# Up and down projection of a decoder layer: one chain of steps that pairs products of neighbouring units

## The chip, the cores and the metric

One core of a Trainium2 chip runs the whole layer. The metric is the device time of one execution in microseconds. Engines are named as the profile names them: PE (TensorE), DVE (VectorE), ACT (ScalarE), POOL (GpSimd) and SP, whose queue issues the DMAs.

## The reference, cut to what matters

The kernel computes one layer of a hybrid decoder for a prompt of 1024 tokens and 8 x 4 sample tokens, 1056 tokens in all. RMSNorm, w_in, the S5 branch, the attention and the gates are untouched by the change. The rest is:

```python
mixed = g_attn * (attn @ p['w_attn_o']) + g_ssm * (ssm @ p['w_ssm_o'])
x = x + mixed @ p['w_out']                                   # 1024 x 1024
hdn = jax.nn.relu(_rmsnorm(x, p['norm2_g']) @ p['w_up'])     # 1024 x 4096
x = x + (hdn * hdn) @ p['w_down']                            # 4096 x 1024
```

## The kernel before

All is fp32 and feature-major: a tile has 128 features on the partitions and T = 1056 tokens along its rows, TH = 528 in each half. An operand of a matmul is split into a rounded part and a rest (hi and lo, ACT's cast and DVE's subtraction), and each product term takes three matmuls (L1068 to L1070).

**w_out** (L1020 to L1045). Eight tiles `m` of 128 features, in the order 0 to 7. Each takes 72 matmuls of 352 columns, then DVE adds the result to x (L1034), ACT squares it (L1035), POOL adds up the squares for the norm (L1037) and the tile `x2_m` is written to `x2_d` (L1038). The left halves of the tiles fill slots 0 and 2 (L1040, L1041).

**up** (L1120 to L1158). The 1024 x 4096 product is cut into 16 units. A unit is one 2 x 2 block product with seven block products instead of eight: sums of the operand's blocks stand in seven *slots* (hi and lo, four tiles `j` each), sums of a unit's weight blocks in seven weight tiles. `prep_sums` loads the four blocks `f` of a unit and makes the sums on POOL (L946 to L949), `prep_split` splits the seven tiles `fw` on ACT (L960) and DVE (L961). `product` is 24 matmuls of 264 columns. The products of a unit go into four pairs of PSUM banks: 0, 3 and 6 one after the other into one bank pair (A or B, in turn), 2 into the other of these, 1 and 4 into C, 5 into D. In up ACT copies intermediate sums into `ua`, `ub`, DVE combines them into the four quarters of two tiles h (L1130), then come the token rsqrt with relu (L1148), the square (L1149), four POOL sums `hc`, `hd` (L1153 to L1156), and seven writes to `h_d` (L1158), since the sums of h are down's slots.

Slots 0 to 3 lie in `slot_hi` and `slot_lo`, slots 4 to 6 in `slot_b`, whose pool opens after w_out. All fills except those of slots 0 and 2 (sums `t`, casts L1090 and L1093, subtractions L1091 and L1094) stand in a loop after w_out (L1098 to L1111). `token_rsqrt_bcast` (L1160) turns the sum of squares into `r2`: matmuls `n_ss` (L150), a chain of small DVE operations (L137 to L154), two diagonal tiles (L161, L165), and matmuls `n_pb` (L169).

**down** (L1187 to L1214). 16 units again: four groups `g` of 1024 hidden features, four pairs `mp` of output tiles in each. All four units of a group use the same seven slots. `load_group` (L1173 to L1185) reads them from `h_d`: 14 transfers `st`, each with an ACT cast (L1184) and a DVE subtraction (L1185), through six staging tiles. The old x comes back as eight tiles `y` (L1168), and DVE adds each product into their quarters (L1194), eight such additions in a unit.

The order on each engine is set by a scheduler at build time, from the order of the program text and the priorities that `high_priority` gives; each engine then runs its own list in that order and waits on semaphores. Four things of the text matter here:

```python
for j in range(4):                 # after w_out: all fills but slots 0 and 2
    ...
for p in range(16):
    up(p, w0 if p == 0 else prep_split(prep_sums(F_UP + p), W5))
for g in range(4):
    load_group(g)                  # all seven slots between two units
    for mp in range(4):
        down(g, mp, prep_split(prep_sums(F_DN + 4 * g + mp), W3))
```

Of the kernel before, what the change touches and what calls it, by code (L numbers as in the profile page):

```python
# [58 lines left out]
def trunk_kernel(ctx, tc, xt, wts, wff, pp_d, cp_d, g1_d, abias, sbias, ckt, cvr, ck_tail, cv_tail,  # L59
# [862 lines left out]
    with ExitStack() as ph2:  # L922
# [16 lines left out]
        def prep_sums(u, ahead=4000):
            with tc.high_priority(offset=ahead):  # L940
                raw = [fwp.tile([P, 512], F32, tag="wr", bufs=7, name=f"f{u}_{i}") for i in range(4)]
                for i in (2, 3, 0, 1):
# [7 lines left out]
            return u, (a11, a21, a12, s2, a22, s4, s1)  # L950

        def prep_split(us, tags, ahead=4000):
            u, xs = us
            out = []
            with tc.high_priority(offset=ahead):
                for i, x in enumerate(xs):
                    tag = tags[_wn[0] % len(tags)]
                    _wn[0] += 1
                    w = (accp if tag[0] == "a" else wpool).tile([P, 2, 512], F32R, tag=tag, name=f"fw{u}_{i}")
                    A.copy(w[:, 0], x)  # L960
                    V.tensor_sub(w[:, 1], x, w[:, 0].bitcast(F32))  # L961
                    out.append(w)
            return out

        with ExitStack() as phs:
# [54 lines left out]
            for m in range(8):  # L1020
                w = load_unit(U_OUT + m)
                x2 = accp.tile([P, T], F32, tag=f"a{m}", name=f"x2_{m}") if m < 4 else (
                    newT if m < 7 else newT2)(f"x2_{m}")
# [4 lines left out]
                if m == 0:
                    gemm_k([blk(w, k) for k in range(8)], macts, pss)
                for c in range(3):  # L1030
                    s = chunks[c]
                    if m:
# [15 lines left out]
        with ExitStack() as phs:
# [8 lines left out]
            def tmp(i, name):  # L1057
                return fp_.tile([P, 2, TH], F32, tag=f"tm{i}", name=name)
# [19 lines left out]
            def halves(t):  # L1078
                return hv(t[:, :TH]), hv(t[:, TH:])

            W3 = ("whi", "wlo", "wraw")
            W5 = ("whi", "wlo", "wraw", "a0", "a1", "whi", "wlo", "wraw", "a2", "a3")
            w0 = prep_split(w0, W3, 1000)
            _wn[0] = 0
            g2n = cpool.tile([P, 8], F32, name="g2n")
            V.tensor_scalar(g2n, C("g2"), -1.0, None, ALU.mult)
            def fill(r, j, src, scale=None):
                hi, lo = slots[r][0][:, j], slots[r][1][:, j]
                if scale is None:
                    A.copy(hi, src)  # L1090
                    V.tensor_sub(lo, src, hi.bitcast(F32))  # L1091
                else:
                    A.activation(hi, src, AF.Copy, scale=scale)  # L1093
                    V.scalar_tensor_tensor(lo, src, scale, hi.bitcast(F32), ALU.mult, ALU.subtract)  # L1094

            for j in range(4):
                xa, xb = x2s[j], x2s[4 + j]
                ga, gb = C("g2", j, j + 1), C("g2", 4 + j, 5 + j)  # L1098
                gan = g2n[:, j : j + 1]
                q1, q2, q3 = [tmp(i, f"t{j}_{i}") for i in range(3)]  # L1100
                b22, t1, t2, t3, t4 = q1[:, 0], q1[:, 1], q2[:, 0], q2[:, 1], q3[:, 0]
                A.activation(b22, xb[:, TH:], AF.Copy, scale=gb)
                V.scalar_tensor_tensor(t3, xa[:, TH:], gan, b22, ALU.mult, ALU.add)
                fill(1, j, t3)
                G.tensor_add(t1, xa[:, :TH], xa[:, TH:])
                V.scalar_tensor_tensor(t2, t1, gan, b22, ALU.mult, ALU.add)
                fill(3, j, t2)
                V.scalar_tensor_tensor(t4, xb[:, :TH], gb, t2, ALU.mult, ALU.add)
# [288 lines left out]
```

## Time and profile before

| | |
|---|---|
| median of 3 runs | 1420.46 us (1417.52 to 1422.59) |
| the profiled execution | 1419.88 us |
| its span | 1418.1 us |
| mean granted clock of TensorE | 0.972 |
| PE, DVE, ACT, POOL busy | 95%, 62%, 36%, 31% of the span |
| up and down, from the last matmul of w_out to the end of the last product | 705.2 to 1413.7 us |

Busy PE is not the same as PE at its peak. The useful number is the cadence of matmuls in a stretch that nothing disturbs, and how far the other stretches fall behind it.

### The profile page before, as it was taken

What the parts mean: (1) busy time and instruction counts of PE and PEld (TensorE: products, weight loads), DVE (VectorE), ACT (ScalarE), POOL (GpSimd) and SP (SyncE); (2) the same over time, 40 slices, a digit from 0 to 9 for tenths busy, and PEclk for the clock granted to TensorE, in tenths of its full rate; (3) what the DMA queues carried; (4) which work ended last, traced back from release to release, by engine and by line L of the source; (5) the groups of instructions that cost most, each with busy time, mean ns of one, the idle gap of its engine ahead of it and who ended that gap; (6) DMA issues with size and microseconds to landing.
All of it is one profiled execution on the core that took longest, in us unless ns stands there. A gap on an engine that the chain in (4) does not pass through costs nothing. (4 is left out here: it accounts for less than half of the span.)

```text
span 1418.1 us, 23479 instructions
## 1 busy us (share of the span) xinstructions
PE 1347.4 (95%) x9405; PEld 1272.7 (90%) x9405; DVE 881.4 (62%) x1401; ACT 505.3 (36%) x843; POOL 442.4 (31%) x348
## 2 busy tenths in 40 slices
PE   7989999999989999999959999999987999999998
PEld 7978999999866659999949999999987999999998
DVE  7969567333467556543497566656657586775953
ACT  6112233223165453222344444434435252432520
POOL 5595322000000000004345665566542233232320
PEclk9999999999989999999969999999998999999999
DMA  6232442331321115423203444344469262452531
GB/s 256 92 86 74 117 89 85 101 114 53 116 92 53 54 44 202 163 92 133 93 8 124 165 152 151 123 159 153 149 240 342 84 234 78 123 183 58 167 107 62
DMA packets 88909, 176.31 MB, mean 124 GB/s; under 512 B 23296, under 2 KB 32512, under 8 KB 88512
## 3 DMA queue, kind: packets, MB, share of 16 engines
q1 hardware_dynamic: 88800, 174.81, 38.1%
q8 instruction: 74, 1.21, 0.3%
q14 instruction: 35, 0.29, 0.1%
HBM read 121.37 MB, written 53.23 MB: 123 GB/s over the span
## 5 line engine op out<-in xcount | busy, mean ns | idle before, releaser
L118 PE MATMUL z<-x_hi,whi 128*128 128x352 f32 x528 | 173.4, 328 | 1.8 <-DVE gs L250 1.8
L120 PE MATMUL z<-x_hi,wlo 128*128 128x352 f32 x528 | 172.2, 327 | 1.5 <-DVE wlo L105 1.5
L119 PE MATMUL z<-x_lo,whi 128*128 128x352 f32 x528 | 172.5, 327 | 0.0
L1037 POOL TENSOR_TENSOR ssq<-ssq,sq 128x352 f32<-128x352 f32 x21 | 23.8, 1135 | 435.1 <-ACT sq L1035 435.1
L960 ACT CAST fw<-f 128x512 fp32r<-128x512 f32 x128 | 79.4, 622 | 167.1 <-PE Dd L1070 34.1
L961 DVE TENSOR_TENSOR fw<-f,fw 128x512 fp32r<-128x512 f32 x128 | 110.8, 867 | 40.8 <-ACT fw L960 40.8
L946 POOL TENSOR_TENSOR f_s<-f,f 128x512 f32<-128x512 f32 x32 | 53.3, 1665 | 217.4 <-DVE fw L961 175.8
L961 DVE TENSOR_TENSOR fw<-f_s,fw 128x512 fp32r<-128x512 f32 x96 | 92.3, 962 | 28.1 <-ACT fw L960 28.0
L120 PEld LDWEIGHTS z<-x_hi,wlo 128*128 128x128 f32 x528 | 99.9, 189 | 4.3 <-issue 2.3
L118 PEld LDWEIGHTS z<-x_hi,whi 128*128 128x128 f32 x528 | 100.5, 190 | 3.1 <-ACT whi L104 2.1
L119 PEld LDWEIGHTS z<-x_lo,whi 128*128 128x128 f32 x528 | 100.6, 191 | 1.7 <-issue 1.3
L104 ACT CAST whi<-wraw 128x1024 fp32r<-128x1024 f32 (+3 forms) x46 | 46.5, 1011 | 153.0 <-PE z L119 90.9
L960 ACT CAST fw<-f_s 128x512 fp32r<-128x512 f32 x96 | 59.7, 621 | 109.2 <-PE Cd L1070 32.3
L105 DVE TENSOR_TENSOR wlo<-wraw,whi 128x1024 fp32r<-128x1024 f32 (+3 forms) x46 | 57.9, 1260 | 12.9 <-ACT whi L104 12.8
L118 PE MATMUL wo<-m_hi,whi 128*128 128x352 f32 x192 | 61.9, 323 | 0.0
L119 PE MATMUL wo<-m_lo,whi 128*128 128x352 f32 x192 | 61.5, 320 | 0.0
L120 PE MATMUL wo<-m_hi,wlo 128*128 128x352 f32 x192 | 61.5, 320 | 0.0
L1068 PE MATMUL Ad<-slot_hi,fw 128*128 128x264 f32 x192 | 56.6, 295 | 4.8 <-ACT slot_hi L1184 3.3
L1153 POOL TENSOR_TENSOR hc<-h 128x528 f32<-128x528 f32 x16 | 21.8, 1363 | 120.9 <-ACT h L1149 120.9
L1069 PE MATMUL Ad<-slot_lo,fw 128*128 128x264 f32 x192 | 56.4, 294 | 2.0 <-DVE slot_lo L1185 2.0
L949 POOL TENSOR_TENSOR f_s<-f_s,f 128x512 f32<-128x512 f32 x32 | 50.6, 1581 | 21.2 <-issue 15.1
L1068 PE MATMUL Au<-slot_hi,fw 128*128 128x264 f32 x192 | 56.2, 293 | 0.7 <-ACT ua L1130 0.7
(420 smaller groups left out, 4647.4 us busy)
## 6 DMA issues: line engine op xcount, KB each, us to landing
f<-in_dram SPq DMA_DIRECT2D x128, 256.0 KB
st<-h_d SPq DMA_DIRECT2D x56, 528.0 KB
wraw<-in_dram SPq DMA_DIRECT2D x42, 512.0 KB
h_d<-h SPq DMA_DIRECT2D x48, 264.0 KB
g_d<-gs SPq DMA_DIRECT2D x16, 528.0 KB
h_d<-hc SPq DMA_DIRECT2D x32, 264.0 KB
h_d<-hd SPq DMA_DIRECT2D x32, 264.0 KB
gr<-y_d SPq DMA_DIRECT2D x8, 528.0 KB
```

What stands on the lines that cost most here:

```text
L104: A.copy(whi[:, s], raw[:, s])
L105: V.tensor_sub(wlo[:, s], raw[:, s], whi[:, s].bitcast(F32))
L118: mm_(out, wh, ah[:, s], start=first, stop=False)
L119: mm_(out, wh, al[:, s], start=False, stop=False)
L120: mm_(out, wl, ah[:, s], start=False, stop=last)
L946: G.tensor_add(s1, a21, a22)
L949: G.tensor_add(s4, s2, a12)
L960: A.copy(w[:, 0], x)
L961: V.tensor_sub(w[:, 1], x, w[:, 0].bitcast(F32))
L1037: G.tensor_add(sacc[:, s], sacc[:, s], sq[:, s])
L1068: mm_(o, wh, ah[:, j, s], start=start and j == 0, stop=False, **k)
L1069: mm_(o, wh, al[:, j, s], start=False, stop=False, **k)
```

## The change

1. The w_out tiles go in the order 0, 4, 1, 5, 2, 6, 3, 7. After a tile of the first four, slots 0 and 6 of that `j` are filled; after a tile of the last four, slots 3 and 1, and `t4`, the operand of slot 4, is written to memory (`t4_d`) because slot 4 lies in the pool that opens later. `slot_hi` now holds slots 0, 6, 3, 1. After w_out only slots 2, 4 (from `t4_d`) and 5 are left to fill.
2. Up and down become 33 steps. Step n runs products 0, 3, 6 of unit n and products 1, 2, 4, 5 of unit n-1, in the order 0, 1', 2', 3, 4', 5', 6 (with a prime those of the unit before). The number of products and of matmuls is the same.
3. The evacuations of up write straight into h, without `ua` and `ub`: four ACT copies and four DVE operations a unit, as before.
4. Down's slots 0, 3, 6 of a group are loaded in the first step of the group, slots 1, 2, 4, 5 in the second, each when its last reader is done. Staging: three `tm` tiles and two others (before: four and two); the tiles `hc`, `hd` share those three. The tiles `y` are loaded two per step.
5. Two of a unit's four weight blocks, needed a step later, lie in a pool of their own of four tiles.

```diff
-            for m in range(8):
+            for i, m in enumerate((0, 4, 1, 5, 2, 6, 3, 7)):
...
+                if m < 4:
+                    fill_a(0, j, xa[:, :TH], ga)
+                    G.tensor_add(t1, xa[:, :TH], xa[:, TH:])
+                    fill_a(6, j, t1, ga)
+                else:
+                    q2 = newT2(f"q2_{j}")
+                    t2, t3 = q2[:, :TH], q2[:, TH:]
+                    with tc.high_priority(offset=40):
+                        A.activation(b22, xb[:, TH:], AF.Copy, scale=gb)
+                        V.scalar_tensor_tensor(t2, t1, gan, b22, ALU.mult, ALU.add)
+                        fill_a(3, j, t2)
+                    V.scalar_tensor_tensor(t3, xa[:, TH:], gan, b22, ALU.mult, ALU.add)
+                    fill_a(1, j, t3)
+                    V.scalar_tensor_tensor(t2, xb[:, :TH], gb, t2, ALU.mult, ALU.add)
+                    nc.sync.dma_start(t4_d[j], t2)
...
-            def tmp(i, name):
-                return fp_.tile([P, 2, TH], F32, tag=f"tm{i}", name=name)
+            def tmp(name):
+                return fp_.tile([P, 2, TH], F32, tag="tm", bufs=3, name=name)
...
+            order = ((0, 0), (1, 1), (1, 2), (0, 3), (1, 4), (1, 5), (0, 6))
+            banks = {0: "X", 1: "C", 2: "Y", 3: "X", 4: "C", 5: "D", 6: "X"}
...
+            def step(n, first, second, tags, ahead=4000):
...
+                for side, r in order:
+                    item = (first, second)[side]
+                    if not item:
+                        continue
+                    k = banks[r]
+                    start = r not in (3, 4, 6)
+                    if start:
+                        ps[k] = psd(tag[k], f"{k}{n}")
+                    product(ps[k], ws[r], r, start)
+                    item["ev"](r, pv(ps[k]))
+                if second and second.get("end"):
+                    second["end"]()
...
             for p in range(16):
-                up(p, w0 if p == 0 else prep_split(prep_sums(F_UP + p), W5))
+                cur = up_item(p)
+                if p:
+                    prep_sums(F_UP + p, fp_)
+                step(p, cur, prev, W6 if p in (0, 15) else W10, 4000 if p else 1000)
+                if p == 0:
+                    r2 = newT2("r2")
...
+                    token_rsqrt_bcast(cpool, lambda n: psd("D", n)[:, 0, :], sacc, dg, r2, "n2")
+                prev = cur
...
-            for g in range(4):
-                load_group(g)
-                for mp in range(4):
-                    down(g, mp, prep_split(prep_sums(F_DN + 4 * g + mp), W3))
+            for n in range(17):
+                cur = None
+                if n < 16:
+                    cur = down_item(n)
+                    if n % 4 == 0:
+                        load_slots(n // 4, (0, 3, 6))
+                    prep_sums(F_DN + n, fp_)
+                if n % 4 == 1:
+                    load_slots(n // 4, (1, 2, 4, 5))
+                step(16 + n, cur, prev, W6)
+                prev = cur
```

The lists of the engines up to w_out are the same in both kernels. Three places show what moved.

ACT at the end of w_out, before (`sq27` is the square of the last tile, L1040 a cast of the w_out loop, L1090 and L1093 the casts of slots after it):

```order
L1035 ACTIVATE sq27_6080<-x2_7_6078 128x352 x2
L1040 ACTIVATE slot_hi_5386<-x2_7_6078,cp_152 128x528
L960 CAST fw0_3_6186<-f0_s1_5970 128x512
L960 CAST fw0_4_6189<-f0_3_5964 128x512
L1102 ACTIVATE t0_0_6200<-x2_4_5775,cp_152 128x528
L1035 ACTIVATE sq27_6080<-x2_7_6078 128x352
L1093 ACTIVATE slot_b_6176<-t0_0_6200,cp_152 128x528
L1090 CAST slot_b_6176<-t0_0_6200 128x528
L1090 CAST slot_hi_5386<-t0_1_6201 128x528 x2
L1102 ACTIVATE t1_0_6218<-x2_5_5871,cp_152 128x528
L960 CAST fw0_6_6195<-f0_s0_5969 128x512
L1090 CAST slot_b_6176<-t0_2_6202 128x528
```

and now (`L1029`, `L1032` are the casts of slots, `fw0` the weights of the first unit):

```order
L1029 CAST slot_hi_5387<-q2_2_5990 128x528 x2
L1058 ACTIVATE sq23_6024<-x2_3_6021 128x352 x2
L1032 ACTIVATE slot_hi_5387<-x2_3_6021,cp_153 128x528
L964 CAST fw0_0_6260<-f0_0_6000 128x512
L964 CAST fw0_3_6263<-f0_s1_6009 128x512
L1058 ACTIVATE sq23_6024<-x2_3_6021 128x352
L1032 ACTIVATE slot_hi_5387<-q1_3_6022,cp_153 128x528
L1058 ACTIVATE sq27_6123<-x2_7_6121 128x352 x2
L964 CAST fw0_2_6420<-f0_1_6001 128x512
L1032 ACTIVATE slot_b_6227<-x2_4_5494,cp_153 128x528
L1032 ACTIVATE slot_b_6227<-x2_5_5698,cp_153 128x528
L1032 ACTIVATE slot_b_6227<-x2_6_5902,cp_153 128x528
```

Before, only slots 0 and 2 were complete at the last square, and 23 casts and copies for the other slots followed (the three sums `t1`, `t2`, `t3` of each `j` among their inputs). Now the casts of slots 3 and 0 stand among the squares, and after the last tile follow those of slot_b, which need no sum.

The DMA queue where up passes into down, before (`y` are the old x, `h_d` the sums of h, `st0_r j` the loads of slot r for the first group):

```order
L1168 DMA y0_10079<-x2_d_76 128x1056
L1158 DMA h_d_77<-hc14_9829 128x528
L943 DMA f17_1_10368<-in_2_dram 128x512
L1158 DMA h_d_77<-hd14_9830 128x528
L1168 DMA y1_10081<-x2_d_76 128x1056
L1158 DMA h_d_77<-hd14_9830 128x528
L1168 DMA y3_10085<-x2_d_76 128x1056
L1183 DMA st0_00_10095<-h_d_77 128x1056
L1168 DMA y4_10087<-x2_d_76 128x1056
L1168 DMA y5_10089<-x2_d_76 128x1056
L1183 DMA st0_02_10099<-h_d_77 128x1056
```

and now:

```order
L1182 DMA h_d_77<-h14_0_9452 128x528
L1182 DMA h_d_77<-hc14_9909 128x528
L1221 DMA st0_00_9926<-h_d_77 128x1056
L1182 DMA h_d_77<-hc14_9909 128x528
L1232 DMA y5_10437<-x2_d_76 128x1056
L1182 DMA h_d_77<-hd14_9910 128x528
L1221 DMA st0_02_9930<-h_d_77 128x1056
L1221 DMA st0_32_9938<-h_d_77 128x1056
L1182 DMA h_d_77<-hd14_9910 128x528
L1221 DMA st0_30_9934<-h_d_77 128x1056
L950 DMA f18_2_10441<-in_2_dram 128x512
```

Five of the eight loads `y` are now ahead of this place (y0 to y4), and slots 0, 3 and 6 come first among the loads; they still stand behind the writes of h14.

DVE at the first change of group, before (L1185 slots, L961 weights, L1194 additions into y):

```order
L1185 TENSOR_TENSOR slot_lo_5387<-st1_12_11027,slot_hi_5386 128x1056
L1185 TENSOR_TENSOR slot_lo_5387<-st1_20_11031,slot_hi_5386 128x1056
L1194 TENSOR_TENSOR y6_10091<-y6_10091,Ad0_3_10836 128x528
L961 TENSOR_TENSOR fw20_1_11089<-f20_2_11073,fw20_1_11089 128x512
L1185 TENSOR_TENSOR slot_lo_5387<-st1_22_11035,slot_hi_5386 128x1056
L1185 TENSOR_TENSOR slot_lo_5387<-st1_30_11039,slot_hi_5386 128x1056
L1194 TENSOR_TENSOR y7_10093<-y7_10093,Bd0_3_10835 128x528
L961 TENSOR_TENSOR fw20_2_11092<-f20_1_11072,fw20_2_11092 128x512
L1185 TENSOR_TENSOR slot_lo_5387<-st1_32_11043,slot_hi_5386 128x1056
L1185 TENSOR_TENSOR slot_b_6176<-st1_40_11047,slot_b_6176 128x1056
L961 TENSOR_TENSOR fw20_3_11095<-f20_s1_11080,fw20_3_11095 128x512
L1194 TENSOR_TENSOR y7_10093<-y7_10093,Cd0_3_10837 128x528
```

and now (L1223 slots, L965 weights, L1125 additions):

```order
L1223 TENSOR_TENSOR slot_lo_5388<-st1_30_10883,slot_hi_5387 128x1056
L1125 TENSOR_TENSOR y7_10657<-y7_10657,X19_10695 128x528
L965 TENSOR_TENSOR fw19_2_10920<-f19_1_10660,fw19_2_10920 128x512
L1223 TENSOR_TENSOR slot_lo_5388<-st1_32_10887,slot_hi_5387 128x1056
L1125 TENSOR_TENSOR y5_10437<-y5_10437,C19_10721 128x528
L965 TENSOR_TENSOR fw20_3_10923<-f20_s1_10908,fw20_3_10923 128x512
L1125 TENSOR_TENSOR y4_10435<-y4_10435,D19_10823 128x528
L965 TENSOR_TENSOR fw19_4_10926<-f19_3_10662,fw19_4_10926 128x512
L1223 TENSOR_TENSOR slot_lo_5388<-st1_60_10891,slot_hi_5387 128x1056
L1125 TENSOR_TENSOR y7_10657<-y7_10657,X19_10695 128x528
L1125 TENSOR_TENSOR y6_10655<-y6_10655,X19_10695 128x528
L965 TENSOR_TENSOR fw19_5_10929<-f19_s2_10669,fw19_5_10929 128x512
```

Before, six of these twelve are subtractions of a slot, two for every weight tile. Now there are three beside four weight tiles, with additions of two products of one unit (C19, D19 belong to unit 18) and of the next (X19) between them.

## Rows read from the trace of the kernel before

**Rows 1.** The page, section 2: busy tenths of TensorE, and the clock granted to it in tenths of full speed, in 40 slices of the span (35.5 us each):

```profile
PE   7989999999989999999959999999987999999998
...
PEclk9999999999989999999969999999998999999999
```

**Rows 2.** Busy time by stretch of the span (us from its start): the length, then busy us (and instructions) of PE, its weight loads, DVE, ACT and POOL, the granted clock (1.00 is full speed), the DMA share and GB/s. The stretches in order: w_out; the start of up; the worst part of that start; up; the passage from up to down; 10 us of that passage; the first change of group with two stretches of 10 us (1150 and 1160) beside it; the second and the third change; down after the last change:

```profile
613.60:705.20 91.60, 91.60 (x577) 91.43 (x576) 32.48 (x46) 25.89 (x45) 27.77 (x24) 1.00 0.31 107
705.20:750.00 44.80, 28.45 (x169) 26.17 (x169) 39.16 (x61) 21.67 (x37) 17.28 (x9) 0.70 0.11 34
720.00:737.00 17.00, 4.73 (x14) 3.21 (x14) 15.04 (x28) 10.08 (x16) 6.07 (x2) 0.50 0.06 15
750.00:1040.00 290.00, 290.00 (x2398) 290.00 (x2398) 180.91 (x190) 119.62 (x191) 173.86 (x116) 1.00 0.44 145
1040.00:1105.00 65.00, 53.78 (x373) 50.44 (x372) 41.23 (x42) 27.21 (x33) 23.04 (x15) 0.87 0.91 316
1060.00:1070.00 10.00, 6.53 (x24) 5.54 (x24) 5.47 (x6) 4.75 (x5) 2.85 (x3) 0.51 0.92 291
1150.00:1160.00 10.00, 10.00 (x85) 10.00 (x84) 10.00 (x12) 6.46 (x9) 0.00 (x0) 1.00 0.89 310
1155.00:1180.00 25.00, 22.77 (x187) 22.56 (x187) 22.94 (x28) 9.89 (x13) 8.56 (x4) 1.00 0.79 278
1160.00:1170.00 10.00, 7.77 (x64) 7.56 (x63) 10.00 (x12) 4.83 (x6) 6.14 (x3) 1.00 1.01 380
1230.00:1262.00 32.00, 29.77 (x234) 29.56 (x233) 29.75 (x33) 16.20 (x21) 9.49 (x5) 0.95 0.81 274
1320.00:1345.00 25.00, 22.77 (x176) 22.56 (x176) 23.83 (x27) 11.06 (x14) 8.54 (x4) 0.93 0.48 165
1345.00:1410.00 65.00, 65.00 (x540) 65.00 (x539) 30.65 (x45) 11.80 (x19) 10.33 (x8) 1.00 0.26 87
```

**Rows 3.** The timeline of PE (start, length, operation, and in brackets the idle time before it and what ended it): three rows from the last matmul of w_out to the first matmul of the token rsqrt's broadcast, then one of the passage from up to down:

```profile
705.00 0.32 PE L120 MATMUL wo<-m_hi,wlo 128*128 128x352 f32 x1
...
729.82 0.59 PE L1068 MATMUL Cu<-slot_hi,fw 128*128 128x264 f32 x1 [5.19 <-ACT slot_hi L1090]
...
745.88 0.32 PE L169 MATMUL n_pb<-diag,ones 128*128 128x352 f32 x1
...
1060.59 0.59 PE L1068 MATMUL Ad<-slot_hi,fw 128*128 128x264 f32 x1 [2.48 <-ACT slot_hi L1184]
```

**Rows 4.** The timeline of the start of up, one row of POOL and seven of DVE, then one of DVE at the first change of group (columns as in group 3):

```profile
712.03 1.74 POOL L948 TENSOR_TENSOR f_s<-f_s,f 128x512 f32<-128x512 f32 x1
712.56 1.77 DVE L1091 TENSOR_TENSOR slot_b<-t,slot_b 128x528 fp32r<-128x528 f32 x1
...
717.32 0.68 DVE L961 TENSOR_TENSOR fw<-f_s,fw 128x512 fp32r<-128x512 f32 x1
...
728.34 0.76 DVE L1103 SCALAR_TENSOR_TENSOR t<-x,g2n,t 128x528 f32<-128x528 f32 x1
...
729.70 0.70 DVE L1091 TENSOR_TENSOR slot_b<-t,slot_b 128x528 fp32r<-128x528 f32 x1
730.32 1.32 DVE L141 TENSOR_TENSOR n_t<-n_i 128x9 f32<-128x9 f32 x1
...
741.41 1.22 DVE L161 TENSOR_TENSOR diag<-cp,n_yh 128x1024 fp32r<-128x1024 f32 x1
...
743.83 0.23 DVE L165 TENSOR_SCALAR diag<-cp,n_yl 128x32 fp32r<-128x32 f32 x1
...
1156.52 1.24 DVE L1185 TENSOR_TENSOR slot_lo<-st,slot_hi 128x1056 fp32r<-128x1056 f32 x1
```

**Rows 5.** The timeline of the DMA queue in the passage from up to down (start, time to issue, line, transfer):

```profile
1040.89 0.36 SPq L1168 DMA_DIRECT2D y<-x_d  x1
...
1053.11 0.32 SPq L1183 DMA_DIRECT2D st<-h_d  x1
...
1060.17 0.32 SPq L1183 DMA_DIRECT2D st<-h_d  x1
```

**Rows 6.** Groups of instructions, five of DVE and one of ACT from 705 us to the end, one of POOL from 600 us: line, engine, operation, shapes, count, then busy us and mean ns of one, then the idle time before them and what ended it:

```profile
L961 DVE TENSOR_TENSOR fw<-f,fw 128x512 fp32r<-128x512 f32 x125 | 108.8, 871 | 40.1 <-ACT fw L960 40.1
L961 DVE TENSOR_TENSOR fw<-f_s,fw 128x512 fp32r<-128x512 f32 x95 | 91.6, 964 | 27.4 <-ACT fw L960 27.3
L1185 DVE TENSOR_TENSOR slot_lo<-st,slot_hi 128x1056 fp32r<-128x1056 f32 x32 | 46.8, 1485 | 8.8 <-ACT slot_hi L1184 8.8
L1148 DVE SCALAR_TENSOR_TENSOR h<-h,r 128x1056 f32<-128x1056 f32 x32 | 41.1, 1320 | 0.0
...
L1194 DVE TENSOR_TENSOR y<-y,Ad 128x528 f32<-128x528 f32 x40 | 27.4, 699 | 31.8 <-PE Ad L1070 31.8
...
L1184 ACT CAST slot_hi<-st 128x1056 fp32r<-128x1056 f32 x32 | 33.5, 1073 | 13.2 <-DMA st<-h_d 10.9 <-PE Bd L1070 2.3
...
L947 POOL TENSOR_TENSOR f<-f,f 128x512 f32<-128x512 f32 x32 | 50.5, 1579 | 1.4
```

**Rows 7.** PE's waits from 1150 to 1180 us (us in total, times, longest):

```profile
PE Dd L1070 <- DVE fw L961: 2.2, 1, 2.2
```

**Rows 8.** The timeline of the end, the last row of DVE and of the DMA queue (columns as in groups 3 and 5):

```profile
1413.72 1.32 DVE L1194 TENSOR_TENSOR y<-y,Bd 128x528 f32<-128x528 f32 x2 [2.20 <-PE Bd L1070]
...
1414.46 0.94 SPq L1214 DMA_DIRECT2D out_dram<-y  x2
```

More of the change, by code (lines that the diff above doesn't have):

```diff
@@ L181, in trunk_kernel @@
     h_d = dpool.tile([7, P, 16, TH], F32, name="h_d")
+    t4_d = dpool.tile([4, P, TH], F32, name="t4_d")
     psx = ctx.enter_context(ExitStack())
@@ L949, in prep_sums, with split_w @@
                 G.tensor_add(s4, s2, a12)
[L950 to L954, printed above, removed]
+            raws[u] = (a11, a21, a12, s2, a22, s4, s1)
+        def split_w(u, i, tags, ahead=4000):
             with tc.high_priority(offset=ahead):
[L956 to L963, printed above, removed]
+                x = raws[u][i]
+                tag = tags[_wn[0] % len(tags)]
+                _wn[0] += 1
+                w = (accp if tag[0] == "a" else wpool).tile([P, 2, 512], F32R, tag=tag, name=f"fw{u}_{i}")
+                A.copy(w[:, 0], x)
+                V.tensor_sub(w[:, 1], x, w[:, 0].bitcast(F32))
+            return w
         with ExitStack() as phs:
@@ L1076, in hv @@
                 return ap.rearrange("p (c t) -> p c t", c=2)
[L1078 to L1094, printed above, removed]
@@ L1096, in trunk_kernel @@
-            for j in range(4):
[L1097 to L1108, printed above, removed]
-                fill(4, j, t4)
-                fill(5, j, b22)
-                fill(6, j, t1, ga)
@@ L1160, in trunk_kernel, with quads @@
[L1160 to L1169 removed]
+            def quads(ta, tb):
+                return [hv(t[:, h * TH : (h + 1) * TH]) for t in (ta, tb) for h in range(2)]
@@ new lines, in trunk_kernel @@
+            for j in range(4):
+                fill(slots[2][0][:, j], slots[2][1][:, j], xbs[j][:, :TH], C("g2", 4 + j, 5 + j))
+            t4s = [tmp(f"t4_{i}") for i in range(2)]
+            for j in range(4):
+                t4 = t4s[j // 2][:, j % 2]
+                nc.sync.dma_start(t4, t4_d[j])
+                fill(slots[4][0][:, j], slots[4][1][:, j], t4)
+            for j in range(4):
+                fill(slots[5][0][:, j], slots[5][1][:, j], xbs[j][:, TH:], C("g2", 4 + j, 5 + j))
@@ L1171, in trunk_kernel, with load_slots @@
+            accs = {}
             _sn = [0]
-            def load_group(g):
+            def load_slots(g, rs):
                 with tc.high_priority(offset=1500):
-                    for r in range(7):
+                    for r in rs:
                         hi, lo = slots[r]
```

222 lines of the change are left out of this document (124 added, 98 removed).

## The prediction

> **What bounds the kernel now.** I read the slices of the page first. PE is near its full tenths everywhere in the second half of the span but in two places, about 700 to 750 us and 1030 to 1100 us, and the granted clock dips there too [rows 1]. Next come the stretches: up from 750 to 1040 us and down after 1345 us show PE busy without a gap at clock 1.00, so PE bounds them. The cadence of the last of them is 65 / 540 = 0.1204 us for a matmul of 264 columns, so a product of 24 costs 2.89 us and seven of them 20.2 us. In w_out a matmul of 352 columns takes 91.6 / 577 = 0.159 us, also without a gap [rows 2]. The change leaves the 32 x 7 x 24 = 5376 matmuls of up and down as they are, so all that it can give back is what the other stretches lose against that cadence. By matmul counts [rows 2]:
>
> - start of up: 44.8 - 169 x 0.1204 = 24.5 us
> - up to down: 65 - 373 x 0.1204 = 20.1 us
> - three changes of group: 25 - 187 x 0.1204 = 2.5, then 32 - 234 x 0.1204 = 3.8 and 25 - 176 x 0.1204 = 3.8, together 10.1 us
>
> That is 54.7 us, the ceiling of the gain apart from the tail. Now what ends last in each. At the start of up PE waits for ACT's casts of slots, the longest time 5.2 us, and the clock falls to 0.50, the lower of the two levels (1.2 and 2.4 GHz), when PE has stood for most of 720 to 737 us [rows 2, 3]. DVE is busy 39.2 of the 44.8 us: fills, weight splits and the token rsqrt queue on one engine [rows 2]. The diagonal tiles are done at 744 us, 39 us after w_out's last matmul, and the first `n_pb` follows at 745.9 [rows 3, 4]. In the passage PE waits for casts of loaded slots at half clock, while the DMA share is 0.91 and eight `y` loads stand in one queue with the first slot loads [rows 2, 3, 5]. At the first change of group DVE is busy 10.00 of 10 us twice and PE waits 2.2 us for a weight tile behind the slots [rows 2, 7].
>
> **The change, part by part.**
>
> *More work inside w_out: nothing.* For each `j`, DVE gets six fill operations of 528 (0.70 to 0.76 us, [rows 4]) in place of the one of slot 2, over four `j` some 14 us, ACT about 10 us and POOL four sums. They join 32.5, 25.9 and 27.8 us of work under 91.6 us of matmuls [rows 2]: DVE would come to 47. The cover is w_out itself; without it these are the very operations that PE waits for now. If two w_out tiles ran into their PSUM banks, at most one addition of 0.5 us would be late, and I take 0.
>
> *Start of up.* In the new list of DVE 46 operations stand between the last addition of w_out and the last diagonal part: 10 weight splits at 0.68, 11 slot operations with a scale at 0.76, 6 without at 0.70, the small ones 3.5 us with one of 1.32, the diagonals 2 x 1.22 + 2 x 0.23 = 2.9 [rows 4]. The 0.68 is a split beside no sum of POOL (the means 0.87 and 0.96 of [rows 6] contain the delayed ones). Sum: 6.8 + 8.4 + 4.2 + 3.5 + 2.9 = 25.8 us. A fill beside a POOL sum took 1.77 instead of 0.70 [rows 4], 1.07 us more, and POOL has nine operations in its list there (two units' sums and the last square). So the diagonals are done between 26 us (none meets) and 36 us (all do) after w_out; I take 32, since now too the sums come early. PE has 144 matmuls of 264 columns ahead of the first `n_pb`, 17.3 us, and 1 to 2 us of `n_ss`. It then stands 32 + 2 - 19 = 15, and I add 1 for the `t4` that go through memory. Loss 16 instead of 24.5: **-8.5**. Ends: diagonals at 26 us, loss 9 or 10, **-15**; at 36 us with later waits of slot 4 behind, loss 21, **-3**. Late next: the rsqrt, no longer the slots.
>
> *Up to down.* Five products of up's last two units need no load of down, 14.5 us of cover that did not exist, since all seven slots were replaced between two units. In the new order slots 0, 3 and 6 have a whole step, 20.2 us, from their last reader. Against this: the first loads stand in the queue behind the writes of h14, whose POOL sums (four at about 1.6, [rows 6]) follow two rsqrt operations of 1.32 us [rows 6] and two squares: 6.4 + 2.6 us, and with squares and write about 13 us after that unit's last product, and `st` waits for `hc`, `hd` in the three shared staging tiles. 13 us, a load (0.54 MB at the passage's 316 GB/s, 1.7 us), a cast of 1.1 and a subtraction of 1.5 us [rows 2, 6], less the 14.5 us of cover, leave some 3 or 4 us for the first product, and as much for the slots of the second step; I take 8 instead of 20.1: **-12**. Ends: 3 and 16, **-17** and **-4**. The eight `y` are spread, two a step, which takes five of them, 2.7 MB, out of the fullest 30 us and is part of this.
>
> *Changes of group.* DVE had the work of a whole group change in one step: 14 slots x 1.4, 7 splits x 0.9, 8 additions x 0.70, some 31 us against 20.2 of PE. Now it is two steps: 14 x 1.4 + 14 x 0.9 + 16 x 0.70 = 43.4 against 40.4 (for the slots between the 1.24 of an undisturbed one and the mean of 1.49, [rows 4, 6]). The 3 us can be carried over the next step, where DVE has 8 free. I take 0.5 for each change instead of 3.4: **-8.6**. Ends: no loss, **-10**, and half of today's, **-5**.
>
> *Tail.* Now the last product ends with two additions, 1.32 us, then the output goes out [rows 8]; the new last product is number 5, with one: **-0.6**.
>
> *The chain itself: 0.* Between the copy out of a bank and the next start in it lie at least two products, 5.8 us, for a copy of about 0.7; the split weights run six to ten tiles ahead as before. At the ends: nothing gained, and up to 0.2 us a step lost (33 steps, 6 us) if the queue's order delays weight loads.
>
> Sum: -8.5 - 12 - 8.6 - 0.6 = -29.7 us, from the profiled execution's 1419.9 to **1390.2 us**; that execution lies 0.6 us under the median of the runs, so I say 1391.
>
> **The rivals.**
>
> 1. *Everything hides.* Passage and changes lose nothing and the diagonals come at 26 us: -15 - 20 - 10 - 0.6 = -46, about **1374**. For it: 14.5 us of cover and PE as the only bound in 290 us of up [rows 2]. Against it: the DVE sum at the start and the queue behind h14.
> 2. *Half of it.* The start saves 3, the passage 4 and the changes 5, with the tail -13: **1407**. For it: DVE already runs 90% there, and loads share 0.91 of the DMA.
> 3. *DVE becomes the bound, slower.* Let every POOL sum hold a DVE operation for 1.07 us, as at 712 us [rows 4]. Two steps around a change then have 14 x 1.24 + 14 x 0.68 + 16 x 0.70 + 8 x 1.07 = 46.6 us of DVE against 40.4: 6.2 us late at each change, 3 us worse than now, and in the passage, where the rsqrt operations and eight sums of `hc`, `hd` come on top, up to 17 us more, so 25 there instead of 20. It decides from 43.8 us of DVE in two steps, where the loss equals today's. With the start saving 3: 9 + 5 - 3 = +11, less the tail, **1430**. The Trainium skill's page "SBUF — State Buffer", section "Who interferes with whom", has such a rule: a DVE instruction with two inputs in SBUF and a GpSimd instruction that reads SBUF share a port pair, and whichever comes second waits for the whole of the first; by that rule alone this case would be the forecast. The pair at 712 us agrees. Against its size: in the change of group at 1150 us POOL ran 0.00 of the 10 us in which DVE was full, because its sums wait for the splits, and the mean split, 0.87 to 0.96, is only a fifth to a quarter of 1.07 above 0.68 [rows 2, 6].
> 4. *The change does not do what it says*: the lists let the stalls return a step later, in sum as before, **1420**. The lists show products and loads alternating, so little speaks for it.
>
> **How the numbers follow.** The forecast's case (saving 20 to 38 us, 1382 to 1400) gets 0.60, rival 1 0.12, rival 2 0.18, rival 3 0.06, rival 4 0.04. A measurement tells 0.3%, 4.3 us, from no change, so faster 0.60 + 0.12 + 0.18 = 0.90, same 0.04, slower 0.06. The range leaves out rivals 3 and 4 and the lower half of rival 1: from 1374 to 1409, with the forecast's ends and rival 2 inside.
>
> **What would show it.** Right: the first `n_pb` about 34 us after w_out's last matmul and PE waiting there for DVE's diagonals, not for casts of slots; in the passage less than 10 us lost and no stretch of 10 us at clock 0.50; DVE under 10.00 of 10 us at the changes, and no wait of PE above 1 us there; up and down otherwise at 0.1204 us a matmul. Wrong: a wait that recurs at every step (weights behind the queue), a passage that still loses 20 us with PE waiting for `st`, or DVE operations of 1.77 us throughout the chain.

## The result

The changed kernel took 1388.94 us (median of 4 runs, 1388.26 to 1389.93) against 1420.55 us before: a ratio of 0.978, 95% interval 0.9761 to 0.9798, 31.6 us less. The forecast was 1391. Its profiled execution took 1389.93 us, span 1388.1 us, mean granted clock 0.984 instead of 0.972.

The page's slices of PE and of its clock, to set beside [rows 1]:

```profile
PE   7979999999999999999989999999997999999998
...
PEclk9999999999989999999999999999999999999999
```

The trough at slice 20 (counted from 0) is shallower, the one at slice 30 is still there, and from slice 12 on none is below 0.9 of the clock. In what follows, every loss is counted in one way: from the end of w_out's last matmul 55 us on (the start), 1020 to 1120 us (the passage), 1120 to 1370 us (the changes of group); length less 0.1204 us for each matmul. Before, these are 24.7, 20.2 and 11.2 us, up to 1.1 above the sums from [rows 2] because the stretches are longer. Stretches of the changed kernel (columns as in [rows 2]; w_out ends at 704.63 us):

```profile
704.63:759.63 55.00, 48.31 (x351) 47.25 (x350) 45.09 (x64) 28.32 (x49) 25.64 (x17) 0.91 0.39 123
1020.00:1120.00 100.00, 91.18 (x714) 89.63 (x714) 74.60 (x81) 40.05 (x54) 42.07 (x26) 0.97 0.67 224
1120.00:1370.00 250.00, 250.00 (x2071) 250.00 (x2070) 187.53 (x225) 93.06 (x126) 66.54 (x44) 1.00 0.43 134
```

55 - 351 x 0.1204 = 12.7, 100 - 714 x 0.1204 = 14.0, 250 - 2071 x 0.1204 = 0.7 us. So the start gave 12.0 us, the passage 6.2, the changes 10.5; the tail (from DVE's last additions, below) 0.8; w_out ended 0.5 us earlier. Together 30.0, which is 1419.88 - 1389.93. PE's waits from 600 us on (total, times, longest):

```profile
PE X L1105 <- DVE y L1125: 4.8, 2, 2.8
PE X L1105 <- ACT h L1125: 3.3, 2, 2.2
PE X L1105 <- ACT slot_hi L1222: 2.2, 1, 2.2
PE n_pb L169 <- DVE diag L165: 1.9, 1, 1.9
PE X L1105 <- ACT fw L964: 1.5, 1, 1.5
```

No wait of 5 us is left, and the longest are for additions of DVE into y, a kind that before shows once, 1.5 us long. At the start, PE's rows that waited (answering to 729.82 and 745.88 of [rows 3]):

```profile
711.85 0.39 PE L1105 MATMUL X<-slot_hi,fw 128*128 128x264 f32 x1 [2.21 <-ACT h L1125]
...
716.42 0.98 PE L150 MATMUL n_ss<-cp,ssq 128*128 128x1 f32 x8 [0.34 <-POOL ssq L1060]
...
729.88 0.39 PE L1105 MATMUL X<-slot_hi,fw 128*128 128x264 f32 x1 [1.07 <-ACT h L1125]
...
735.22 0.40 PE L169 MATMUL n_pb<-diag,ones 128*128 128x352 f32 x1 [1.92 <-DVE diag L165]
```

The 2.2 us and 1.1 us are for the copies out of the first unit's bank pair; the broadcast starts at 735.22, 30.6 us after w_out. The stretch up to there (columns as in [rows 2]):

```profile
704.63:735.22 30.59, 23.90 (x165) 22.84 (x163) 29.52 (x46) 18.84 (x33) 15.28 (x9) 0.89 0.47 147
```

30.59 - 165 x 0.1204 = 10.7 us, so most of the start's 12.7 us is lost here. In the passage:

```profile
1050.34 0.59 PE L1105 MATMUL X<-slot_hi,fw 128*128 128x264 f32 x1 [2.19 <-ACT slot_hi L1222]
...
1058.31 0.36 PE L1105 MATMUL X<-slot_hi,fw 128*128 128x264 f32 x1 [2.81 <-DVE y L1125]
...
1066.35 0.36 PE L1105 MATMUL X<-slot_hi,fw 128*128 128x264 f32 x1 [2.00 <-DVE y L1125]
...
1084.41 0.39 PE L1105 MATMUL X<-slot_hi,fw 128*128 128x264 f32 x1 [1.53 <-ACT fw L964]
```

The first is for the second half of slot 0, the next two for banks that DVE has not emptied. Busy time there in 5 us, and at the three changes in 30 us (columns as in [rows 2]):

```profile
1040.00:1045.00 5.00, 5.00 (x43) 4.96 (x42) 2.58 (x4) 2.12 (x3) 3.31 (x3) 1.00 0.95 320
1045.00:1050.00 5.00, 3.15 (x26) 2.93 (x25) 2.42 (x4) 0.78 (x1) 0.00 (x0) 1.00 0.96 350
1055.00:1060.00 5.00, 2.19 (x19) 2.01 (x18) 5.00 (x6) 2.72 (x4) 5.00 (x3) 1.00 1.00 364
1060.00:1065.00 5.00, 4.35 (x36) 4.13 (x35) 5.00 (x3) 2.37 (x4) 4.84 (x4) 1.00 1.03 339
1130.00:1160.00 30.00, 30.00 (x251) 30.00 (x250) 30.00 (x34) 15.11 (x19) 9.95 (x6) 1.00 0.70 223
1210.00:1240.00 30.00, 30.00 (x251) 30.00 (x250) 29.88 (x32) 15.86 (x21) 10.45 (x7) 1.00 0.72 225
1290.00:1320.00 30.00, 30.00 (x251) 30.00 (x250) 29.41 (x33) 16.29 (x20) 12.09 (x8) 1.00 0.45 139
```

From 1040 to 1050 us the DMA engines are full and DVE is half idle; ten us later DVE is full and PE waits. At the changes DVE is about as full as before ([rows 2], 1150 and 1160 us), 29.4 to 30.0 of 30 us, but PE loses nothing and the wait of [rows 7] is gone. The end of the kernel, DVE's last row, answers to [rows 8]:

```profile
1384.49 0.70 DVE L1125 TENSOR_TENSOR y<-y,D 128x528 f32<-128x528 f32 x1 [1.25 <-PE D L1107]
```

One addition instead of two; from its start to the end of the span 3.6 us instead of 1418.1 - 1413.72 = 4.4.

### The profile page after: what moved, and what is told of

Its sections match the earlier page's. It is cut to its first block, busy times and chain, and to the rows that moved or that the text cites. A ratio compares the mean times of both kernels' runs of the same rounds, so it can differ in the third digit from the quotient of the medians.

```text
span 1388.1 us, 23493 instructions
## 1 busy us (share of the span) xinstructions
PE 1336.7 (96%) x9405; PEld 1265.8 (91%) x9405; DVE 894.6 (64%) x1401; ACT 505.7 (36%) x843; POOL 433.3 (31%) x348
## 4 chain that ended last, share of the span: by engine, by line
PE 76%; DVE 7%; DMA 3%; issue 2%; ACT 1%; POOL 1%; SPq 0%; DVEq 0%; ACTq 0%; POOLq 0%
PE X L1105 6%; PE X L1106 6%; PE X L1107 6%; PE C L1106 4%; PE C L1105 4%; PE C L1107 4%; PE z L118 4%; PE z L119 4%; PE z L120 4%; PE wo L118 2%; PE wo L119 2%; PE wo L120 2%; PE D L1105 2%; PE D L1106 2%; PE D L1107 2%; PE Y L1106 2%
## 5 line engine op out<-in xcount | busy, mean ns | idle before, releaser
L1105 PE MATMUL X<-slot_hi,fw 128*128 128x264 f32 x768 | 221.5, 288 | 12.5 <-DVE y L1125 4.8
L1107 PE MATMUL X<-slot_hi,fw 128*128 128x264 f32 x768 | 220.4, 287 | 0.5 <-DVE fw L965 0.4
L1106 PE MATMUL X<-slot_lo,fw 128*128 128x264 f32 x768 | 220.3, 287 | 0.0
L1105 PEld LDWEIGHTS X<-slot_hi,fw 128*128 128x128 f32 x768 | 147.6, 192 | 13.9 <-issue 5.2
L1107 PEld LDWEIGHTS X<-slot_hi,fw 128*128 128x128 f32 x768 | 146.9, 191 | 0.9 <-DVE fw L965 0.9
L1106 PEld LDWEIGHTS X<-slot_lo,fw 128*128 128x128 f32 x768 | 147.5, 192 | 0.0
L965 DVE TENSOR_TENSOR fw<-f,fw 128x512 fp32r<-128x512 f32 x128 | 119.2, 933 | 28.6 <-ACT fw L964 28.5
L1066 POOL TENSOR_TENSOR q<-x 128x528 f32<-128x528 f32 x4 | 5.8, 1438 | 391.4 <-DVE x L1057 391.4
L965 DVE TENSOR_TENSOR fw<-f_s,fw 128x512 fp32r<-128x512 f32 x96 | 85.7, 893 | 39.3 <-ACT fw L964 39.2
L952 POOL TENSOR_TENSOR f_s<-f,f 128x512 f32<-128x512 f32 x32 | 44.7, 1396 | 167.6 <-DMA f<-in_dram 131.2
L1105 PE MATMUL Y<-slot_b,fw 128*128 128x264 f32 x256 | 73.2, 286 | 0.0
L1106 PE MATMUL Y<-slot_b,fw 128*128 128x264 f32 x256 | 73.2, 286 | 0.0
L1107 PE MATMUL Y<-slot_b,fw 128*128 128x264 f32 x256 | 73.2, 286 | 0.0
```

The costliest lines, as they stand in the source:

```text
L1105: mm_(o, wh, ah[:, j, s], start=start and j == 0, stop=False, **k)
L1106: mm_(o, wh, al[:, j, s], start=False, stop=False, **k)
L1107: mm_(o, wl, ah[:, j, s], start=False, stop=j == 3, **k)
```

## The experiments

Losses by place in us, from each kernel's profile, and the median of its runs:

| kernel | start | passage | changes | median us |
|---|---|---|---|---|
| before | 24.7 | 20.2 | 11.2 | 1420.6 |
| changed | 12.7 | 14.0 | 0.7 | 1388.9 |
| the same again (e12) | 12.7 | 13.7 | 0.5 | 1391.2 |
| e1 new fills only | 9.1 | 19.5 | 12.8 | 1404.4 |
| e2 chain only | 28.3 | 13.2 | 0.7 | 1405.3 |
| e3 four slots without DVE's part | 12.7 | 10.4 | 0.7 | 1387.8 |
| e7 no late writes of h | 12.7 | 9.5 | 0.7 | 1387.5 |
| e10 both e3 and e7 | 12.9 | 4.2 | 0.7 | 1380.2 |
| e6 no POOL sums of five units | 9.0 | 9.5 | 0.7 | 1382.3 |
| e5 four staging tiles | 10.9 | 11.4 | 0.7 | 1385.8 |
| e8 late rsqrt | 11.2 | 11.1 | 0.7 | 1386.0 |
| e9 early copy | 12.1 | 12.1 | 0.5 | 1388.5 |
| e11 e5, e8 and e9 | 10.7 | 9.1 | 0.7 | 1388.2 |

In e8 and e11 up itself (760 to 1020 us) lost 0.7 us more than in the changed kernel. The program ahead of w_out is the same everywhere and w_out itself runs without a stall, yet in these profiles it ended between 702.7 and 708.5 us. That scatter is in every total, so a difference of 3 us between two totals says little; the losses by place of one and the same kernel repeat within 0.4 us (the changed kernel and e12).

### Which part gives what

e1 takes the new w_out loop with its early fills, and the units as before (shown against the changed kernel):

```diff
-                step(p, cur, prev, W6 if p in (0, 15) else W10, 4000 if p else 1000)
+                up(p, w0 if p == 0 else prep_split(prep_sums(F_UP + p), W5))
...
-                step(16 + n, cur, prev, W6)
+                    down(g, mp, prep_split(prep_sums(F_DN + 4 * g + mp), W3))
```

> The new order of w_out with the early fills of slots 0, 6, 3, 1 and the reload of t4, but up and down as before, unit after unit, with all seven slots of a group loaded between two units. Theory (the gains belong to their places: the start's to the fills, the passage's and the changes' to the chain): the start of up loses about 12 to 15 us instead of 24.5, the passage still 20, the three changes still 10; about 1408 to 1411 us. Rival (the start is helped by the chain, which asks for three products of one unit and four of the next before slots 2, 4, 5): the start still loses 20 us or more, 1416 us or more.

e2 takes the old w_out loop and the old loop of fills, and the chain:

```diff
-            for i, m in enumerate((0, 4, 1, 5, 2, 6, 3, 7)):
+            for m in range(8):
...
+            for j in range(4):
+                xa, xb = x2s[j], x2s[4 + j]
...
+                fill(6, j, t1, ga)
```

> The old order of w_out with all fills but those of slots 0 and 2 after it, and up and down as the chain. Theory: the start loses as much as before (24 us or more, since the chain asks for slots 0, 3, 6 first, which need the sums t1 and t2), the passage about 14 and the changes nothing, as in the changed kernel; about 1403 us. Rival (the chain helps the start): the start loses 12 to 16 us, about 1390 to 1394 us.

The stretches of e1, then of e2 (start, passage, changes):

```profile
708.39:763.39 55.00, 50.41 (x381) 48.95 (x380) 45.83 (x67) 28.45 (x49) 24.21 (x15) 0.94 0.29 93
1020.00:1120.00 100.00, 88.20 (x669) 85.12 (x668) 59.90 (x69) 35.99 (x47) 32.21 (x23) 0.93 0.66 228
1120.00:1370.00 250.00, 243.30 (x1970) 242.68 (x1969) 176.05 (x218) 92.85 (x124) 74.77 (x48) 0.98 0.42 136
```

```profile
705.99:760.99 55.00, 37.18 (x222) 34.30 (x221) 48.62 (x68) 27.17 (x47) 28.93 (x17) 0.78 0.23 63
1020.00:1120.00 100.00, 92.76 (x721) 90.68 (x720) 72.81 (x76) 40.50 (x55) 45.49 (x28) 0.97 0.71 235
1120.00:1370.00 250.00, 250.00 (x2071) 250.00 (x2070) 187.63 (x228) 95.94 (x128) 76.46 (x48) 1.00 0.46 139
```

e1: 1404.35 us, ratio 0.9888 (0.9865 to 0.9910). e2: 1405.25 us, 0.9887 (0.9864 to 0.9909). Against the median of before in their session, 1421.0, they gain 16.7 and 15.8, together 32.5, and the whole change gained 31.6: the two parts add. The theory stands: fills give the start, the chain the changes and a third of the passage. e1 lost less at the start than expected (9.1, not 12 to 15) and so came out under its 1408 to 1411 us. And both expectations missed one thing. The start loses 9.1 with the fills alone and 12.7 with the chain on top, 24.7 as before and 28.3 with the chain: the chain *costs* 3.6 us at the start, with either set of fills.

### What holds the passage

e3 leaves out DVE's subtraction for four slots of the first group:

```diff
+                            if g or r in (0, 3, 6):
                                 V.tensor_sub(lo[:, s], st, hi[:, s].bitcast(F32))
```

> The changed kernel without the DVE subtraction of the rest (lo) for slots 1, 2, 4, 5 of the first group of down, so these four slots keep an old rest: 8 operations of about 1.3 us, 10.5 us, less for DVE in the passage from up to down; loads, casts and matmuls stay. Theory (the 13.8 us that the passage still loses are DVE's, which is full from 1050 to 1090 us): the passage loses 5 to 9 us, 1381 to 1385 us. Rival (the loads come late: they stand behind the writes of h in the queue, at a DMA share of 0.9): 13 to 14 us as now, 1388 to 1389 us.

The passage lost 10.4: more than the theory wanted (5 to 9) and less than its rival (13 to 14). The median, 1387.8, lies by the rival's. e7 takes the writes away instead:

```diff
-                    for r, x in enumerate((b11, t3, b21, t2, t4, b22, t1)):
+                    for r, x in enumerate((b11, t3, b21, t2, t4, b22, t1)) if p < 13 else ():
...
-                            nc.sync.dma_start(st, h_d[r, :, 4 * g + j : 4 * g + j + 2, :])
+                            nc.sync.dma_start(st, h_d[r, :, 4 * min(g, 2) + j : 4 * min(g, 2) + j + 2, :])
```

> The changed kernel without the 21 writes of h for units 13 to 15 of up (5.7 MB); the last group of down reads the rows of the third in their place. POOL's sums, all loads and all matmuls stay. Theory (the loads of the first group are late because they stand behind these writes in the one queue and share full DMA engines with them): the passage loses 3 to 8 us instead of 14.0, with no wait for a cast of slot 0 above 1 us; 1378 to 1384 us. Rival (DVE and POOL are the limit in the passage): it still loses 11 us or more, 1386 to 1389 us.

9.5 us, again between the two, with the median, 1387.5, in the rival's range: the wait for slot 0 is gone, as the theory said, but DVE was busy 8.8 instead of 5.0 us from 1040 to 1050 (columns as in [rows 2]):

```profile
1040.00:1050.00 10.00, 10.00 (x85) 10.00 (x84) 8.77 (x8) 4.27 (x5) 5.52 (x4) 1.00 0.85 271
```

and PE's waits above 0.75 us are all for DVE's additions (its timeline):

```profile
1054.37 0.36 PE L1105 MATMUL X<-slot_hi,fw 128*128 128x264 f32 x1 [1.77 <-DVE y L1125]
...
1065.35 0.39 PE L1105 MATMUL X<-slot_hi,fw 128*128 128x264 f32 x1 [0.81 <-DVE y L1125]
...
1070.01 0.36 PE L1105 MATMUL Y<-slot_b,fw 128*128 128x264 f32 x1 [1.36 <-DVE y L1125]
```

e10 does both:

> Both reliefs of the passage at once: without the writes of h for units 13 to 15 (the last group reads the third's rows) and without the DVE subtraction for slots 1, 2, 4, 5 of the first group (they keep an old rest). Alone the two left the passage at 9.5 and 10.4 us. Theory (two limits stand behind each other there: loads that land late at full DMA engines, and a DVE that is full once they have landed, so that either relief alone mostly shows the other): the passage loses 2 to 6 us, 1376 to 1382 us. Rival (a third limit, such as the order of products on PE or POOL's sums, holds it): 9 us or more, 1384 us or more.

Its passage, with the columns of [rows 2]:

```profile
1020.00:1120.00 100.00, 96.74 (x796) 96.16 (x795) 69.39 (x82) 45.52 (x60) 42.85 (x27) 1.00 0.60 195
```

100 - 796 x 0.1204 = 4.2 us. Single reliefs of 3.6 and 4.5 us, 9.8 together: with the loads on time (e7) the relief of DVE is worth 5.3 us more, and with DVE relieved (e3) the relief of the loads 6.2. So there are two limits: loads that land late, and a DVE that has to do in 30 us what it could not begin in the 10 us before. That each hides part of the other is less sure, since edits of the start alone move the passage by 1.9 to 2.9 us (e9 and e8, below) and the sum of the single reliefs is 8.1. When the loads land can be seen in ACT's casts of the first two loads (start, length, idle before), in the changed kernel and in e10:

```profile
1041.86 1.08 ACT L1222 CAST slot_hi<-st 128x1056 fp32r<-128x1056 f32 x1 [4.24 <-DMA st<-h_d]
...
1049.22 1.07 ACT L1222 CAST slot_hi<-st 128x1056 fp32r<-128x1056 f32 x1 [5.24 <-DMA st<-h_d]
```

```profile
1038.96 1.08 ACT L1222 CAST slot_hi<-st 128x1056 fp32r<-128x1056 f32 x1 [2.15 <-DMA st<-h_d]
...
1043.29 1.08 ACT L1222 CAST slot_hi<-st 128x1056 fp32r<-128x1056 f32 x1 [2.73 <-DMA st<-h_d]
```

7.4 us between the two halves of slot 0, against 4.3. e5 gives one more staging tile, and one tile less to the held weight blocks, so that the second load need not wait for `hc14` to be written:

```diff
-                        return pool.tile([P, 512], F32, tag="wh", bufs=4, name=n)
+                        return pool.tile([P, 512], F32, tag="wh", bufs=3, name=n)
...
-                return fp_.tile([P, 2, TH], F32, tag="tm", bufs=3, name=name)
+                return fp_.tile([P, 2, TH], F32, tag="tm", bufs=4, name=name)
```

> The changed kernel with four tm tiles in place of three (and three tiles for the held weight blocks in place of four, to make room), so that the second load of slot 0 of the first group need not wait for the tile of hc14. Theory (the passage's loss begins with loads that come late: PE waits for the second half of slot 0 at 1050 us, and DVE, half idle from 1040 to 1050 us, is then behind): the passage loses 8 to 11 us instead of 14.0. Rival (the DMA engines are full at a share of 0.95, more staging brings nothing sooner): 13 to 14 us. All in all 1385 to 1389 us.

The first loads in the DMA queue (columns as in [rows 5]) of the changed kernel, then of e5, and e5's first two casts:

```profile
1036.45 0.47 SPq L1221 DMA_DIRECT2D st<-h_d  x1
...
1042.62 0.80 SPq L1221 DMA_DIRECT2D st<-h_d  x2
```

```profile
1035.64 0.98 SPq L1221 DMA_DIRECT2D st<-h_d  x2
```

```profile
1042.11 1.08 ACT L1222 CAST slot_hi<-st 128x1056 fp32r<-128x1056 f32 x1 [2.03 <-DMA st<-h_d]
1043.53 1.08 ACT L1222 CAST slot_hi<-st 128x1056 fp32r<-128x1056 f32 x1 [0.34 <-DMA st<-h_d]
```

In the changed kernel the second load is issued 6.2 us after the first, in e5 right behind it; the casts come 1.4 us apart instead of 7.4, and PE's wait for slot 0 falls from 2.2 to 0.8 us. So the second half of slot 0 was late for want of a staging tile, and not, as the rival had it, for the full DMA engines. What that is worth is less clear: the passage lost 11.4, just above the theory's range, and e8 and e9, which edit the start alone, show 11.1 and 12.1. That e5's gain is its staging is not shown.

### What holds the start

e6 leaves POOL's sums of five units out:

```diff
+                if u - F_UP in (1, 2, 16, 17, 18):
+                    raws[u] = (a11, a21, a12, a11, a22, a12, a21)
+                    return
                 G.tensor_add(s1, a21, a22)
```

> The changed kernel without POOL's four sums of the weight blocks for units 1 and 2 of up and 0 to 2 of down, whose products then use blocks in place of sums; loads, splits and matmuls stay. It takes 8 POOL operations out of the start and 12 out of the passage. Theory (a DVE operation with two inputs from SBUF is held by a POOL sum, about 1 us each): at the start the diagonals are done 5 to 8 us earlier and the start loses 7 to 10 us instead of 12; the passage 9 to 12 instead of 13.8; together 1380 to 1384 us. Rival (the sums matter little, DVE is full by its own operations): within 2 us of the changed kernel, 1387 to 1389 us.

The start lost 9.0, the passage 9.5, as the theory said; so in the passage POOL's sums are worth as much as either relief above. The diagonals were done 27.8 us after w_out instead of 32.9. The seven fills of slots, a small operation of the rsqrt and the last diagonal's part, in the changed kernel and in e6:

```profile
705.96 7.90 DVE L1033 SCALAR_TENSOR_TENSOR slot_b<-x,cp,slot_b 128x528 fp32r<-128x528 f32 x7
...
723.18 1.28 DVE L137 TENSOR_SCALAR n_i<-n_a 128x9 int32<-128x9 int32 x1
...
736.27 1.26 DVE L165 TENSOR_SCALAR diag<-cp,n_yl 128x32 fp32r<-128x32 f32 x1
```

```profile
709.81 4.84 DVE L1036 SCALAR_TENSOR_TENSOR slot_b<-x,cp,slot_b 128x528 fp32r<-128x528 f32 x7
...
721.15 0.15 DVE L137 TENSOR_SCALAR n_i<-n_a 128x9 int32<-128x9 int32 x1
...
736.06 0.23 DVE L165 TENSOR_SCALAR diag<-cp,n_yl 128x32 fp32r<-128x32 f32 x1
```

Seven fills take 7.90 us beside POOL's sums and 4.84 without. 9.0 is also about what e1 loses, whose POOL works 9.5 us from 705 to 740 us and not the changed kernel's 18.7, since the chain asks for the weights of the second and third unit earlier. But it is not the seven fills that this spares. In e1 they met a sum too:

```profile
710.29 8.62 DVE L1030 SCALAR_TENSOR_TENSOR slot_b<-x,cp,slot_b 128x528 fp32r<-128x528 f32 x7
```

They took longer than in the changed kernel, and still e1's diagonals were done 25.3 us after w_out. So why the chain costs 3.6 us at the start stays open. Later sums that meet the rsqrt are one candidate (its operation of 1.28 us above takes 0.16 in e1); the other is that the first step's three products share one bank pair. The latter is what e9 tried, by the order of four casts and one copy on ACT (in e9 and e8 the loop that fills slots 2, 4 and 5 also moves behind the first step in the text):

```diff
+                    c = A.activation(hi, src, AF.Copy, scale=scale)
+                    tc.add_manual_dep(
+                        c.ins, first_copy[0].ins.name,
...
-                        out(A.copy, c11, x)
+                        first_copy.append(out(A.copy, c11, x))
```

> The changed kernel with the first copy out of bank pair X put ahead of the four casts of slot 5 on ACT. Theory (the first step has only products 0, 3 and 6, which share one bank pair, so PE waits 2.2 us for that copy, the clock halves, and the chain's start pays for it): the wait at product 3 is below 0.8 us and the start loses 9 to 11 us instead of 12.7. Rival (the time until the diagonals sets the loss, whatever waits come before it): 12 to 13 us, with a longer wait at the broadcast.

PE's timeline at its start, the two longest waits:

```profile
716.36 0.98 PE L150 MATMUL n_ss<-cp,ssq 128*128 128x1 f32 x8 [2.78 <-POOL ssq L1070]
...
720.05 0.59 PE L1116 MATMUL X<-slot_lo,fw 128*128 128x264 f32 x1 [2.39 <-DVE slot_lo L1040]
```

e9 lost 12.1 us: the wait for the copy is gone, and these two, for the last square's sum and for a slot, stand in its place. That is the rival's number, but not its longer wait at the broadcast, which was 0.9 us. e8 moves the rsqrt behind the second step's products:

```diff
-                    token_rsqrt_bcast(cpool, lambda n: psd("D", n)[:, 0, :], sacc, dg, r2, "n2")
...
                 def end():
+                    if not R2:
+                        R2.append(late_rsqrt())
```

> The changed kernel with the token rsqrt issued after the products of the second step instead of the first, which moves its broadcast matmuls some 70 matmuls down PE's list. Theory (the start's remaining 12.7 us end at the diagonals, as forecast): the start loses 8 to 11 us. Rival (the waits ahead of it set the loss, and the half clock that follows them): 12 to 13 us as now.

e8 lost 11.2, and 0.7 later in up: it gained less than the theory wanted, and PE's wait for the first copy grew from 2.2 to 3.2 us. e11 has e5's, e8's and e9's edits together; e12 is the changed kernel once more:

> The changed kernel, whole, with the three small mends together: four tm tiles, the rsqrt after the second step, the first copy ahead of slot 5's casts. If their effects add (1.8, 1.5 and 0.6 us at their places): the start loses 8 to 11 us, the passage 10 to 13, 1382 to 1387 us. If one wait only takes the place of another: as the changed kernel, 1387 to 1390 us.

> The changed kernel itself once more, for the scatter of the losses by place and for a comparison on one chip. If the passage's loss of 11.1 and 12.1 us in two runs that changed only the start is scatter, it lies between 11 and 14 here, the start at 12 to 13, the changes of group below 1; 1387 to 1390 us. If it is 14.0 again, those two runs moved the passage through the scheduler's lists.

On one chip e11 took 1388.22 us (0.9781, 0.9764 to 0.9799) and the changed kernel 1391.22 (0.9794, 0.9772 to 0.9815): the profile loses some 6 us less in up and down, but the intervals overlap, so a gain in time is unclear, and the median lies in the range for waits that take each other's place. e12's time lies 1.2 us above its range. Its losses, 12.7, 13.7 and 0.5, are near the first profile's, which speaks for the lists and against scatter as what moved the passage in e8 and e9; but 13.7 also lies in the range given for scatter, and two profiles are few.

## Why the prediction was right, and where by luck

The mechanism was right in the main: the start, the passage and the changes each gave time, the passage least surely. That the time came within 2 us of the forecast is luck, because the terms were wrong in opposite ways: the start gave 3.5 us more than forecast and the changes 1.9, the passage 5.8 less.

- *Start of up*: -8.5 forecast, -12.0 measured. The diagonals came 32.9 us after w_out, forecast 32. The failing step is "It then stands 32 + 2 - 19 = 15": PE stood 1.9 us there. The first broadcast matmul needs only the first diagonal, done at 735.2, and the second diagonal's matmul stands 20 matmuls further down, so it came at 30.6 and not at 34. And the matmuls ahead of it, put at 19 us, took 28.7: five waits there, which the forecast put at nothing, add up to 4.8 us, and the granted clock was 0.69 from 712 to 722 us, behind the wait of 2.2 us. A loss of the forecast's order thus came by another path. The us added for `t4` was not there: no wait for slot 4 is left.
- *Up to down*: -12 forecast, -6.2 measured. The loads came late about as worked out, the second one for its staging tile (e5). The failing step is "as much for the slots of the second step": I counted only the loads, and not that DVE, half idle while they were late, must then do slots, splits, the two rsqrt operations and additions at once. DVE as the bound, rival 3's limit, is real here but not at the changes; e10 shows both limits. "Less than 10 us lost" failed with it; that no stretch of 10 us there would fall to clock 0.50 held, the lowest was 0.83 (1050 to 1060 us).
- *Changes of group*: -8.6 forecast, -10.5 measured, all that was there. That DVE would stay under 10.00 of 10 us was wrong; it did not matter, as PE waited for none of it.
- *Tail*: -0.6 and -0.8. *Work in w_out and the chain in between*: 0 and 0; up loses 0.9 us in some 260 in both kernels. DVE was busy 49.5 of w_out's 91.6 us, forecast 47.
- Rival 1 was out by the passage, rival 2 by the start and the changes, rival 4 by all. Rival 3 needed a loss from DVE's hold at every change, and none came. The Trainium skill's rule on the page "SBUF — State Buffer", section "Who interferes with whom", that the second of two such instructions waits for the whole of the first, agrees in kind with the fills' 7.90 against 4.84 us; as a forecast of the total it fails, for at the changes PE lost nothing beside a DVE busy 29.4 to 30.0 of 30 us.

## What to carry to other kernels

Cut a handover into steps so that half of the operands are replaced while the other half is used: an engine that is full for 30 us then costs nothing, where the same work in one step cost 3 to 4 us. Before pricing a stall by its last wait, list the next one: here late loads and a full DVE stood in line, each worth some 4 us alone and 5 or 6 once the other was gone. And look for what a step needs *first* in a chain of producers; a consumer that can start on the first part is not late by the whole.

## What was not expected of the hardware

- An operation of DVE on nine columns took 1.28 us beside a POOL sum and 0.15 without (both shown above): the hold does not scale with the small operation. It is a TENSOR_SCALAR; the Trainium skill's page "SBUF — State Buffer", section "Who interferes with whom", names that kind among those that can take the shared ports.
- The hold works both ways. In e6, POOL's last two additions of squares (its timeline), the first with DVE idle, the second beside the slot operations that follow the seven fills on DVE (714.57 to 717.30 us), took 0.94 and 3.38 us. PE waited 4.6 us for the second; the hold is 2.4 of that, and the square itself came only at 714.06 us, behind seven casts of slots on ACT.

```profile
706.06 0.94 POOL L1063 TENSOR_TENSOR ssq<-ssq,sq 128x352 f32<-128x352 f32 x1 [2.45 <-ACT sq L1061]
714.69 3.38 POOL L1063 TENSOR_TENSOR ssq<-ssq,sq 128x352 f32<-128x352 f32 x1 [7.69 <-ACT sq L1061]
```

- The program up to w_out's end took 702.7 to 708.5 us in thirteen profiles, with w_out never stalled. Where these 6 us come from is open; no experiment was made on that part.
